# A transformer block on one core: where the second gate's modulation is computed, which engine adds the activation sums, and when weight sums are stored

## The chip, the cores and the metric

The kernel runs on one core of a Trainium2 chip. The core has five engines with their own instruction queues: PE (TensorE, matrix products), DVE (VectorE) and ACT (ScalarE) for elementwise work, POOL (GpSimd), and SP (SyncE), which here issues nearly all transfers between HBM and the on-chip memory (SBUF). Matrix products land in a second memory, PSUM. The metric is the device time of one execution in microseconds (us); less is better. The profile is a hardware trace of one execution.

## The reference

One layer on 512 latent tokens (a grid of 8 rows of 64) and 256 context tokens, 1024 channels, all in 32-bit floats. Cut to what matters here:

```python
mod = silu(c) @ w_ada + b_ada                      # 6 x 1024 values
sh1, sc1, gt1, sh2, sc2, gt2 = split(mod, 6)
h = modulate(rms_norm(x), sh1, sc1)
mix = token_mixer(h, hc, ...)                      # attention, gated linear attention, merge, w_out
x = x + gt1 * mix
h = modulate(rms_norm(x), sh2, sc2)
val, gate = split(h @ w_up, 2)                     # 2 x 2816 columns
gate = depthwise_conv_grid(gate, conv_w, conv_b)   # 3x3 on the 8 x 64 grid
x = x + gt2 * ((gelu(gate) * val) @ w_down)        # 2816 -> 1024
out = rms_norm(x, final_g)
```

`gt2`, the second gate, is needed only where the down projection's result is added.

## The kernel before

**Products.** Every weight and activation of a large product is split into a high part (a cast by ACT, `whi` or `s`) and a low part (the rest, a subtraction, `wlo` or `s`; `split`, line 142, takes POOL unless told otherwise), and three products high-high, high-low, low-high are added up in PSUM (`mm3`). Calls of an engine go through a wrapper, so that nearly all instructions bear line 91 or 90 in the profile; they are told apart by the names of their tiles.

**Stages.** Behind attention and gated linear attention comes the merge (eight steps `j`, from about 405 us): branch projections, gates, and in between the loads of `w_out` (`load_wo`, line 1339). `w_out_norm(t)` (line 1409) then makes the output projection for one of four tiles of 128 tokens, adds it to the residual `x2` and normalises it (`xn`); `transposed(t, xn)` (line 1428) turns it into the columns `h2h`, `h2l`. Then the up projection runs over 22 tiles of 128 hidden columns, tiles 0 to 2 ahead of the loop and 3 to 21 in it, from about 550 to 800 us. The down projection and the last norm follow.

**One tile of the up projection.** `up_weights(i)` (line 1346) loads two pieces of `w_up` (512 KB each, tile `raw`, three buffers) and splits them with POOL (four pairs `whi`, `wlo`). `up_mm` makes 2 x 8 x 3 = 48 products of 512 columns into two PSUM banks, gate and value (`pb`, four in all). `up_out(i)` (line 1476) makes the convolution: one ACT instruction and eight steps on DVE from PSUM into `ac`; then GELU on ACT, and the product with the value half on DVE. Only then are the two banks free for the tile after the next.

**Sums ahead of the down projection.** The down projection of tiles 0 to 17 is done with a scheme of seven products of 2 x 2 blocks. It takes sums and differences of activations and of weights. The activation sums of a pair of tiles are made in `up_out`: one on the even tile in `edge` (one buffer of five pieces of 256), three on the odd tile in `edge` and `second`, all on DVE, and then `edge` is split. The weight sums are made by `weight_sums(n)` (line 1516): two loads of `w_down` into `rawd` (two buffers), two subtractions on DVE, two on POOL; two stores into HBM (`ws`), from where the down projection fetches them. They run at tiles 6, 8, ..., 20 and 21 (`SUM_AT`, line 27), loads and stores in the same tile; `tc.issue_after(load[0].ins)` puts their transfers behind the newest up load on SP's queue.

**The second gate.** `gt2` begins as the bias row in all 128 partitions (line 1470). At tiles 6, 10, 14 and 18 `mod_part` (line 247) makes 256 columns of `silu(c) @ w_ada` as one partial sum in each partition: two loads into `raw`, and eight DVE steps into `mp`. One tile later `mod_bcast` (line 298) adds the 128 partitions on PE with a matrix of ones into a `pb` bank, and DVE adds the result to `gt2`.

**Order.** The program is traced in the order of its text; a planner with a timeline model then orders the instructions of each engine, and each engine runs its list in that order. Work traced earlier has precedence.

Of the kernel before, what the change touches and what calls it, by code (L numbers as in the profile page):

```python
# [23 lines left out]
NF = FF // 128  # L24
NL = 4
NP = (NF - NL) // 2
SUM_AT = [6, 8, 10, 12, 14, 16, 18, 20, 21]
EPS = 1e-6
ATT_SCALE = 96.0 ** -0.5
GQ_SCALE = 128.0 ** -0.5  # L30
# [43 lines left out]
def block_kernel(ctx: ExitStack, tc: tile.TileContext, p, out):  # L74
# [40 lines left out]
    def p2():  # L115
        return tl(psp, [128, 1024], F32, "p2", 2)
# [1211 lines left out]
    hbm = ctx.enter_context(tc.tile_pool(name="hbm", bufs=1, space=bass.MemoryType.DRAM))  # L1328
    x2_ = [tl(hbm, [128, 1024], F32, f"x2_{t}") for t in range(4)]
    sums_ = [tl(hbm, [128, 2048], F32, f"ws_{i}") for i in range(NP)]  # L1330
    emf_ = tc.tile_pool(name="emf", bufs=1)
    emf = emf_.__enter__()
    x2 = [tl(emf, [128, 1024], F32, f"x2{t}") for t in range(4)]
# [4 lines left out]

    def load_wo(k, tile_=raw_tile):
        r = tile_()  # L1340
        SY.dma_start(out=r, in_=w_out[:, k, :])
        h_, l_ = S4([128, 1024]), S4([128, 1024])
        split(h_, l_, r, V if k in (5, 7) else G)
        wo.append((h_, l_))
# [11 lines left out]
    with tc.tile_pool(name="emg", bufs=1) as em_:  # L1356
        def merge_weights(j):
            return (split_w(load_cols(w_in, CGB + j * 128)), split_w(load_cols(w_brg, j * 128, k1=4), 512))

        def mraw():  # L1360
            return tl(em_, [128, 1024], F32, "xn", 3)


        gsum = p2()
        ahead = merge_weights(0)
        for j in range(8):
            wgb, wbg = ahead
            gb = pb()
            proj(wgb, gb)
            if j + 1 < 8:  # L1370
                ahead = merge_weights(j + 1)
            bg = pb()
            for k in range(4):
                bg_ = mm3(bg, k3(wbg[0], 4, 128)[:, k, :], k3(wbg[1], 4, 128)[:, k, :], yT[k][:, 0, :], yT[k][:, 1, :], k == 0,
                    k == 3)
            sg = tl(em_, [128, 512], F32, "sg", 2)
            si = sigmoid(sg, gb)
            tt(V, sg, bg, sg, ALU.mult)
            tt(V, sg, sg, m1[j // 2][:, j % 2, :], ALU.add)
            mg[j] = S4([128, 2, 512])  # L1380
            split(mg[j][:, 0, :], mg[j][:, 1, :], sg, V)
            if j in (1, 2, 3, 5):
                load_wo(len(wo), mraw)
            if j == 0:
                mod_end()
            with tc.issue_after(load[0].ins):
                if j < 4:
                    mod_part(2048 + j * 256, gsum[:, j * 256:j * 256 + 256], mraw)
                elif j == 4:
                    mod_begin(mraw, p2()[:, 0:256])  # L1390
            if j == 6:
                m_, gh, gl = mp_tile(), *[tl(em_, [128, 1024], F32R, "xn", 3) for _ in range(2)]
                with tc.issue_after(si.ins):
                    A.copy(m_, begun[7])
                    A.copy(gh, gsum)
                sub(V, gl, gsum, f(gh))
            elif j == 7:
                with tc.issue_after(bg_.ins):
                    mod_fin(7, m_)
                    gp = p2()  # L1400
                    for half in range(2):
                        hs = slice(half * 512, (half + 1) * 512)
                        total(gp[:, hs], gh[:, hs], gl[:, hs])
                        tt(V, gt1[:, hs], gt1[:, hs], gp[:, hs], ALU.add)
        for k in range(4, 8):
            load_wo(k)
        h2h = [S4([128, 2, 512]) for _ in range(4)]
        h2l = [S4([128, 2, 512]) for _ in range(4)]
        def w_out_norm(t):
            cs = slice(t * 128, (t + 1) * 128)  # L1410
            mp = p2()
            for k in range(8):
                for half in range(2):
                    hs = slice(half * 512, (half + 1) * 512)
                    mm3(mp[:, hs], mg[k][:, 0, cs], mg[k][:, 1, cs], wo[k][0][:, hs], wo[k][1][:, hs], k == 0, k == 7)
            xn = mraw()
            for half in range(2):
                hs = slice(half * 512, (half + 1) * 512)
                tt(V, xn[:, hs], mp[:, hs], gt1[:, hs], ALU.mult)
                tt(V, x2[t][:, hs], x2[t][:, hs], xn[:, hs], ALU.add)  # L1420
            s2 = sm(1, "s2")
            A.activation(xn, x2[t], AF.Square, accum_out=s2)
            A.dma_start(out=x2_[t], in_=x2[t])
            r2 = rstd_exp(s2, 1, 1.0 / D)
            V.tensor_scalar(out=xn, in0=x2[t], scalar1=r2, scalar2=None, op0=ALU.mult)
            return xn

        def transposed(t, xn):
            cs = slice(t * 128, (t + 1) * 128)
            for kk in range(2):  # L1430
                tp = pb()
                for k in range(4):
                    PE.transpose(tp[:, k * 128:(k + 1) * 128], xn[:, (4 * kk + k) * 128:(4 * kk + k + 1) * 128], ident)
                ht = tl(em_, [128, 4, 128], F32, "ht2", 2)
                for k in range(4):
                    kt = 4 * kk + k
                    V.tensor_scalar(out=ht[:, k, :], in0=tp[:, k * 128:(k + 1) * 128], scalar1=modsc2[:, kt:kt + 1],
                                    scalar2=modsh2[:, kt:kt + 1], op0=ALU.mult, op1=ALU.add)
                for k in range(2):
                    split(h2h[2 * kk + k][:, :, cs], h2l[2 * kk + k][:, :, cs], ht[:, 2 * k:2 * k + 2, :], V)  # L1440


        n0 = w_out_norm(0)
        n1 = w_out_norm(1)
        transposed(0, n0)
        n0 = w_out_norm(2)
        transposed(1, n1)
        n1 = w_out_norm(3)
        w0 = [up_weights(i) for i in range(2)]
        z0 = p2()  # L1450
        ps0 = [(z0[:, 0:512], z0[:, 512:1024]), (pb(), pb())]
        up_mm(w0[0], ps0[0], 0, 256)
        transposed(2, n0)
        up_mm(w0[1], ps0[1], 0, 256)
        transposed(3, n1)
        w0.append([])
        for c0 in (FF + 256, 256):
            h_, l_ = S4([128, 1024]), S4([128, 1024])
            split(h_, l_, load_cols(w_up, c0))
            w0[2].append((h_, l_))  # L1460
        z0 = p2()
        ps0.append((z0[:, 0:512], z0[:, 512:1024]))
        up_mm(w0[2], ps0[2], 0, 256)
        for i in range(3):
            up_mm(w0[i], ps0[i], 256, 512)
# [1 line left out]

    emf_.__exit__(None, None, None)
    kept = ctx.enter_context(tc.tile_pool(name="kept", bufs=1))
    gt2 = tl(kept, [128, 1024], F32, "gt2")  # L1470
    SY.dma_start(out=gt2, in_=p["b_ada"][0:1, 5120:6144].broadcast_to([128, 1024]))
    first, second, hid, gelu, edge = [], [], {}, [], [None]

    with tc.tile_pool(name="eff", bufs=1) as ef:

        def up_out(i, ps):
# [23 lines left out]
            elif i % 2 == 0:  # L1500
                edge[0] = tl(ef, [128, 1280], F32, "edge", 1)
                z = grp(edge[0], 5)
                tt(V, z[:, 0::4, :], grp(vp, 2), grp(ac, 2), ALU.mult)
                sub(V, z[:, 2, :], z[:, 0, :], z[:, 4, :])
            else:
                z = grp(edge[0], 5)
                second.append(tl(kept, [128, 768], F32, "second", NP))
                q = grp(second[-1], 3)
                tt(V, q[:, 0::2, :], grp(vp, 2), grp(ac, 2), ALU.mult)
                tt(V, z[:, 1, :], z[:, 4, :], q[:, 2, :], ALU.add)  # L1510
                sub(V, z[:, 3, :], z[:, 1, :], z[:, 0, :])
                sub(V, q[:, 1, :], q[:, 0, :], z[:, 3, :])
                first.append((S4([128, 1024]), S4([128, 1024])))
                split(*first[-1], edge[0][:, 0:1024], V if i > 1 else G)

        def weight_sums(n):

# [1 line left out]
            for i in range(2):  # L1519
                SY.dma_start(out=r[i], in_=w_down[:, 2 * n + i, :])  # L1520
            b11, b12, b21, b22 = [z[:, x:x + 512] for z in r for x in (0, 512)]
            sub(V, b11, b12, b11)
            sub(V, b12, b22, b12)
            sub(G, b22, b22, b11)
            sub(G, b21, b21, b22)
            return r
# [2 lines left out]
            up_out(i, ps0[i])  # L1529
        for i in range(3, NF):  # L1530
            w = up_weights(i)
            if i in (6, 10, 14, 18):
                part = mod_part(5120 + (i - 6) * 64, mp_tile(), raw_tile)
            ps = (pb(), pb())
            up_mm(w, ps, 0, 512)
            up_out(i, ps)

            if i in (7, 11, 15, 19):
                mod_bcast(part, gt2[:, (i - 7) * 64:(i - 3) * 64])
            if i in SUM_AT:  # L1540
                n = SUM_AT.index(i)
                with tc.issue_after(load[0].ins):
                    for k, r in enumerate(weight_sums(n)):
                        SY.dma_start(out=sums_[n][:, k * 1024:k * 1024 + 1024], in_=r)

        raws, fg = [0], tl(ef, [128, 1280], F32, "edge", 1)[:, 0:1024]

# [49 lines left out]
        for n in range(NP):  # L1597
# [12 lines left out]
            if n in (2, 4, 6, 8):  # L1610
                r = load_down(NF - NL + n // 2 - 1)
                wl_.append((S4([128, 1024]), S4([128, 1024])))
                split(*wl_[-1], r)
            if n == NP - 3:
                bw.append(back_weights(0))
        u1, u2, u7, c22 = halves(S4f()), halves(S4f()), halves(S4f()), halves(S4f())
# [141 lines left out]
```

## Time and profile before

| | us |
|---|---|
| time, median of 3 runs | 926.18 (925.3 to 931.43) |
| profiled execution, time | 926.52 |
| profiled execution, span of the trace | 924.7 |
| DVE busy | 703.1 (76% of the span) |
| ACT busy | 409.6 |
| POOL busy | 354.5 |
| PE busy between 557.6 and 802 us | 214.07 of 244.40 |
| DVE busy there | 224.43 of 244.40 |
| POOL busy there | 110.02 of 244.40 |

A row of the trace gives a start, a duration, an engine, an operation, what it writes and reads by tile, and in brackets how long the engine had been idle before it and what it waited for. Groups of instructions give a count, the busy time in us, the mean of one in ns, and the idle time before them. In tables by window the columns are the window, its length, and the busy time and count of PE, weight loads, DVE, ACT and POOL; then the granted PE clock (1.00 is full), the DMA share and the rate.

### The profile page before, as it was taken

The numbers are of one execution on the slowest core, as the hardware profiler recorded it, in microseconds if no ns is written. First come the engines' busy times: TensorE is split into PE (matmuls) and PEld (weight loads), VectorE is DVE, ScalarE is ACT, GpSimd is POOL, SyncE is SP. The second block draws the span as 40 slices with busy tenths as digits, with TensorE's granted clock in tenths as the row PEclk, the third lists the DMA queues.
The fourth block names the chain that finished last, engine by engine and source line by source line (L and its number), as shares of the span: only waits on it lengthen the run. The fifth ranks groups of instructions, "written<-read, shape, count | busy, mean of one in ns | idle before, by whom it ended". The sixth has DMA issues, their size and how long they took to land.

```text
span 924.7 us, 12841 instructions
## 1 busy us (share of the span) xinstructions
PE 875.9 (95%) x4798; PEld 740.7 (80%) x4798; DVE 703.1 (76%) x1089; ACT 409.6 (44%) x664; POOL 354.5 (38%) x220
## 2 busy tenths in 40 slices
PE   7999999999999999999999999996996969999996
PEld 5788899888888888888888998775784858787785
DVE  5487788867877776646746849998989899877857
ACT  4465667745354545345544334232232223355424
POOL 2512373532524343336634234354453444222005
PEclk9999999999999999999999999999897989999998
DMA  9950001152415151449726224645636556557612
GB/s 295 318 148 1 1 12 28 66 143 95 128 35 146 38 148 44 129 147 303 244 86 188 91 78 151 201 131 169 205 138 204 168 153 249 167 190 267 244 33 92
DMA packets 141791, 131.07 MB, mean 142 GB/s; under 512 B 7962, under 2 KB 123010, under 8 KB 141728
## 3 DMA queue, kind: packets, MB, share of 16 engines
q1 hardware_dynamic: 140496, 127.19, 44.7%
q10 hardware_dynamic: 832, 2.40, 0.7%
q8 instruction: 38, 0.62, 0.3%
q0 software_dynamic: 400, 0.65, 0.2%
q14 instruction: 25, 0.20, 0.1%
HBM read 116.39 MB, written 13.63 MB: 141 GB/s over the span
## 4 chain that ended last, share of the span: by engine, by line
PE 63%; DVE 17%; issue 7%; DMA 7%; ACT 3%; POOL 2%; SPq 0%; DVEq 0%; ACTq 0%; POOLq 0%
PE pb L91 27%; PE p L91 17%; PE pb L90 14%; PE p L90 6%; DVE ac L91 5%; DVE mp L91 3%; DMA raw<-in_w_ada_dram 3%; DMA rawd<-in_w_down_dram 2%; DVE s L91 2%; DVE edge L91 2%; DVE second L91 1%; POOL wlo L91 1%; ACT s L91 1%; DMA raw<-in_w_down_dram 1%; DVE wlo L91 1%
## 5 line engine op out<-in xcount | busy, mean ns | idle before, releaser
L91 POOL TENSOR_TENSOR wlo<-raw,whi 128x1024 fp32r<-128x1024 f32 (+1 forms) x88 | 196.4, 2242 | 283.8 <-ACT whi L91 253.4
L91 PE MATMUL pb<-s,whi 128*128 128x512 f32 (+1 forms) x906 | 277.4, 389 | 29.3 <-DVE ac L91 27.9
L91 PEld LDWEIGHTS pb<-s,whi 128*128 128x128 f32 x906 | 169.8, 192 | 65.9 <-issue 31.2
L91 PE MATMUL pb<-s,wlo 128*128 128x512 f32 (+1 forms) x453 | 175.2, 387 | 0.0
L91 ACT CAST whi<-raw 128x1024 fp32r<-128x1024 f32 (+1 forms) x105 | 101.7, 971 | 140.0 <-DMA raw<-in_w_up_dram 42.1
L91 DVE SCALAR_TENSOR_TENSOR ac<-pb,cwT,ac 128x441 f32<-128x441 f32 (+2 forms) x160 | 110.3, 691 | 5.4 <-ACT ac L91 2.3
L90 PE MATMUL pb<-s,whi 128*128 128x512 f32 x320 | 101.1, 394 | 0.0
L91 PEld LDWEIGHTS pb<-s,wlo 128*128 128x128 f32 x453 | 86.6, 191 | 17.1
L91 PE MATMUL p<-s,s 128*128 128x512 f32 (+1 forms) x398 | 84.5, 364 | 2.1 <-DVE s L91 2.0
L91 PEld LDWEIGHTS p<-s,s 128*128 128x128 f32 x398 | 66.9, 189 | 14.7 <-DVE s L91 3.1
L90 PEld LDWEIGHTS pb<-s,whi 128*128 128x128 f32 x320 | 59.3, 188 | 11.5
L90 PE MATMUL pb<-s,wlo 128*128 128x512 f32 x160 | 62.8, 392 | 0.0
L91 ACT ACTIVATE ac<-ac 128x512 f32<-128x512 f32 x22 | 13.9, 632 | 108.7 <-DVE ac L91 108.7
L91 PE MATMUL p<-whi,s 128*128 128x512 f32 x168 | 56.2, 393 | 0.0
L91 POOL TENSOR_TENSOR s<-raw,s 128x1024 fp32r<-128x1024 f32 (+1 forms) x10 | 23.9, 2401 | 80.7 <-ACT s L91 80.7
L91 PE MATMUL pb<-whi,s 128*128 128x512 f32 x164 | 53.7, 390 | 0.0
L91 PE MATMUL pb<-s,s 128*32 128x128 f32 (+2 forms) x340 | 46.3, 319 | 0.9 <-DMA s<-in_w_ada_dram 0.9
L91 DVE TENSOR_TENSOR pl<-pb,ph 128x512 fp32r<-128x512 f32 x48 | 33.0, 687 | 12.7 <-ACT ph L91 12.3
L91 PE MATMUL p<-kT,s 128*128 128x512 f32 (+1 forms) x192 | 41.2, 350 | 0.9 <-ACT P L91 0.9
L91 PEld LDWEIGHTS pb<-s,s 128*128 128x128 f32 (+1 forms) x340 | 36.1, 159 | 6.7 <-DVE rv L91 1.2
L91 DVE SCALAR_TENSOR_TENSOR mp<-raw,csilu,mp 128x256 f32<-128x256 f32 x35 | 35.0, 1001 | 6.4 <-DMA raw<-in_w_ada_dram 6.0
L91 PE MATMUL p<-s,whi 128*128 128x256 f32 (+1 forms) x156 | 38.6, 338 | 0.0
(269 smaller groups left out, 1695.1 us busy)
## 6 DMA issues: line engine op xcount, KB each, us to landing
raw<-in_w_up_dram SPq DMA_DIRECT2D x44, 512.0 KB, 4.8
raw<-in_w_in_dram SPq DMA_DIRECT2D x28, 512.0 KB, 4.1
rawd<-in_w_down_dram SPq DMA_DIRECT2D x21, 512.0 KB, 5.9
s<-in_w_ada_dram SPq DMA_DIRECT2D x20, 512.0 KB, 6.2
raw<-in_w_ada_dram SPq DMA_DIRECT2D x18, 512.0 KB, 6.7
ws<-rawd SPq DMA_DIRECT2D x18, 512.0 KB, 2.6
xn<-in_w_ada_dram SPq DMA_DIRECT2D x10, 512.0 KB, 5.0
raw<-in_w_down_dram SPq DMA_DIRECT2D x9, 512.0 KB, 4.1
```

The lines of the kernel that those rows point to most:

```text
L90: return fn(*args, **kw)
L91: ins = fn(*args, **kw)
```

## The change

The modulation parts of `gt2` leave the up loop. `gt2` is made earlier, in a pool of its own: cleared, with the bias in partition 0 only. `gate_part(j)` loads 2 x 512 KB of `w_ada` into buffers of its own (`wa`, two) and adds eight DVE steps into 256 columns of `gt2`. Part 0 is placed at step 6 of the merge, part 1 behind the last `w_out` loads, parts 2 and 3 between the first token tiles of the output projection. The sum over partitions is made once, in the up loop at tile 12: `gt2` is split and summed by four products (`total`), and ACT copies the result back.

The activation sums go from DVE to POOL; the split of the first pair goes from POOL to DVE. The weight sums are loaded at tiles 4, 6, ..., 20 and stored one tile later; for the first the DVE subtractions go to POOL. The split of the last four down weights goes from POOL to DVE.

```diff
+    gate_ = ctx.enter_context(tc.tile_pool(name="gate", bufs=1))
+    gt2 = tl(gate_, [128, 1024], F32, "gt2")
+    V.memset(gt2, 0.0)
+    SY.dma_start(out=gt2[0:1, :], in_=p["b_ada"][0:1, 5120:6144])
...
     def load_wo(k, tile_=raw_tile):
         r = tile_()
-        SY.dma_start(out=r, in_=w_out[:, k, :])
+        load[0] = SY.dma_start(out=r, in_=w_out[:, k, :])
...
+        def gate_part(j):
+            acc = gt2[:, j * 256:j * 256 + 256]
+            for k0 in (0, 4):
+                r3 = k3(tl(em_, [128, 1024], F32, "wa", 2), 4, 256)
+                SY.dma_start(out=r3, in_=w_ada[:, k0:k0 + 4, 5120 + j * 256:5376 + j * 256])
+                for k in range(4):
+                    V.scalar_tensor_tensor(out=acc, in0=r3[:, k, :], scalar=csilu[:, k0 + k:k0 + k + 1], in1=acc,
+                                           op0=ALU.mult, op1=ALU.add)
...
+            ahead_ = load[0].ins
             if j in (1, 2, 3, 5):
                 load_wo(len(wo), mraw)
             if j == 0:
                 mod_end()
-            with tc.issue_after(load[0].ins):
+            with tc.issue_after(ahead_):
...
+            if j == 6:
+                with tc.issue_after(load[0].ins):
+                    gate_part(0)
         for k in range(4, 8):
             load_wo(k)
+        with tc.issue_after(load[0].ins):
+            gate_part(1)
...
         n0 = w_out_norm(0)
+        gate_part(2)
         n1 = w_out_norm(1)
+        gate_part(3)
         transposed(0, n0)
...
-    gt2 = tl(kept, [128, 1024], F32, "gt2")
-    SY.dma_start(out=gt2, in_=p["b_ada"][0:1, 5120:6144].broadcast_to([128, 1024]))
...
-                sub(V, z[:, 2, :], z[:, 0, :], z[:, 4, :])
+                sub(G, z[:, 2, :], z[:, 0, :], z[:, 4, :])
...
-                tt(V, z[:, 1, :], z[:, 4, :], q[:, 2, :], ALU.add)
-                sub(V, z[:, 3, :], z[:, 1, :], z[:, 0, :])
-                sub(V, q[:, 1, :], q[:, 0, :], z[:, 3, :])
+                tt(G, z[:, 1, :], z[:, 4, :], q[:, 2, :], ALU.add)
+                sub(G, z[:, 3, :], z[:, 1, :], z[:, 0, :])
+                sub(G, q[:, 1, :], q[:, 0, :], z[:, 3, :])
                 first.append((S4([128, 1024]), S4([128, 1024])))
-                split(*first[-1], edge[0][:, 0:1024], V if i > 1 else G)
+                split(*first[-1], edge[0][:, 0:1024], V)
...
-            sub(V, b11, b12, b11)
-            sub(V, b12, b22, b12)
+            sub(V if n else G, b11, b12, b11)
+            sub(V if n else G, b12, b22, b12)
...
-            if i in (6, 10, 14, 18):
-                part = mod_part(5120 + (i - 6) * 64, mp_tile(), raw_tile)
...
-            if i in (7, 11, 15, 19):
-                mod_bcast(part, gt2[:, (i - 7) * 64:(i - 3) * 64])
-            if i in SUM_AT:
-                n = SUM_AT.index(i)
+            if i == 12:
+                gh, gl = split_w(gt2, eng=V)
+                gp = p2()
+                for hs in (slice(0, 512), slice(512, 1024)):
+                    total(gp[:, hs], gh[:, hs], gl[:, hs])
+                A.copy(gt2, gp)
+            n = (i - 4) // 2
+            if 0 <= n < NP:
                 with tc.issue_after(load[0].ins):
-                    for k, r in enumerate(weight_sums(n)):
-                        SY.dma_start(out=sums_[n][:, k * 1024:k * 1024 + 1024], in_=r)
+                    if i % 2 == 0:
+                        made = weight_sums(n)
+                    else:
+                        for k in range(2):
+                            SY.dma_start(out=sums_[n][:, k * 1024:k * 1024 + 1024], in_=made[k])
...
-                split(*wl_[-1], r)
+                split(*wl_[-1], r, V)
```

More of the change, by code (lines that the diff above doesn't have):

```diff
@@ L26 @@
 NP = (NF - NL) // 2
-SUM_AT = [6, 8, 10, 12, 14, 16, 18, 20, 21]
 EPS = 1e-6
```

## The prediction

> **What bounds the kernel now.** I read the first part of the page, then the chain of work that ended last in order of time, then PE's own waits, then the windows and the timeline around one of those waits.
>
> ```profile
> span 924.7 us, 12841 instructions
> ...
> PE 875.9 (95%) x4798; PEld 740.7 (80%) x4798; DVE 703.1 (76%) x1089; ACT 409.6 (44%) x664; POOL 354.5 (38%) x220
> ```
>
> PE (TensorE) is busy for 95% of the span, so the 5% in which it is not are what a change of order can win. In the chain PE alone carries the stretch of the merge; its first long piece also gives the price of one 512-column matmul at full clock, 66.12 / 296 = 0.223 us.
>
> ```profile
> 409.07 66.12 PE pb L91 x296
> ```
>
> One tile of the up projection is 48 such matmuls, 10.7 us; a pair of tiles is 21.4 us. PE's waits between 555 and 802 us, where the up projection runs, have one dominant row:
>
> ```profile
> PE pb L91 <- DVE ac L91: 28.9, 5, 8.9
> ```
>
> Five waits for the depthwise convolution on DVE (VectorE), 28.9 us, the longest 8.9. Windows around them:
>
> ```profile
> 593.00:616.00 23.00, 21.97 (x97) 17.89 (x97) 21.99 (x25) 5.71 (x8) 10.13 (x5) 1.00 0.65 205
> ...
> 649.00:694.00 45.00, 45.00 (x191) 36.91 (x190) 40.83 (x47) 12.47 (x15) 22.58 (x11) 0.95 0.53 176
> ...
> 704.00:749.00 45.00, 45.00 (x188) 36.50 (x189) 41.38 (x48) 13.11 (x16) 22.58 (x11) 0.95 0.53 175
> ...
> 758.50:800.00 41.50, 40.62 (x168) 32.90 (x169) 37.43 (x49) 13.55 (x17) 17.88 (x9) 0.95 0.73 241
> ```
>
> Columns: window, its length, busy time of PE, weight loads, DVE, ACT (ScalarE), POOL (GpSimd), the granted clock, the DMA share, GB/s. The windows begin behind a long wait each (the first behind a short one). PE is full in them, but behind the long waits the granted clock is 0.95 on average where it was 1.00 in the first: a wait costs its idle time and some slow matmuls after it. DVE is at 91 to 96%. Here is how one wait comes about:
>
> ```profile
> 627.97 3.26 SPq L91 DMA_DIRECT2D ws<-rawd  x2
> 638.20 0.38 SPq L91 DMA_DIRECT2D raw<-in_w_ada_dram  x1
> 638.67 9.90 SPq L91 DMA_DIRECT2D raw<-in_w_up_dram  x4
> ...
> 630.84 5.00 POOL L91 TENSOR_TENSOR wlo<-raw,whi 128x1024 fp32r<-128x1024 f32 x2
> 644.93 2.34 POOL L91 TENSOR_TENSOR wlo<-raw,whi 128x1024 fp32r<-128x1024 f32 x1 [9.09 <-ACT whi L91]
> ...
> 631.08 2.50 DVE L91 TENSOR_SCALAR mp<-raw,csilu 128x256 f32<-128x256 f32 x1
> 644.98 2.58 DVE L91 SCALAR_TENSOR_TENSOR mp<-raw,csilu,mp 128x256 f32<-128x256 f32 x1
> ...
> 643.81 1.04 ACT L91 CAST whi<-raw 128x1024 fp32r<-128x1024 f32 x1 [11.39 <-DMA raw<-in_w_up_dram]
> ...
> 648.29 1.19 PE L91 MATMUL pb<-s,whi 128*128 128x512 f32 x2 [8.75 <-DVE ac L91]
> ```
>
> In SP's queue (SyncE's, which issues the loads) the stores of the weight sums stand ahead of the second modulation load, and that ahead of four loads of up weights; so the cast at 643.81 waited 11.39 us for its weights. On DVE the modulation (tile mp) sits among the convolutions. The mp instruction at 644.98 took 2.58 us while a POOL subtraction ran from 644.93 for 2.34; then the convolution ended and PE went on at 648.29. There are four modulation parts in this stage (tiles 6, 10, 14, 18), one per four tiles, and that is the beat of the waits.
>
> **The change, part by part.** The instructions of the stage, grouped by line and form (busy us, mean ns of one), and the page's row for the convolution:
>
> ```profile
> L91 DVE SCALAR_TENSOR_TENSOR ac<-pb,cwT,ac 128x441 f32<-128x441 f32 (+2 forms) x160 | 110.3, 691 | 5.4 <-ACT ac L91 2.3
> ```
>
> ```profile
> L91 DVE SCALAR_TENSOR_TENSOR mp<-raw,csilu,mp 128x256 f32<-128x256 f32 x28 | 31.6, 1130 | 3.2 <-DMA raw<-in_w_ada_dram 2.9
> ...
> L91 DVE TENSOR_TENSOR edge<-edge 128x256 f32<-128x256 f32 x18 | 22.5, 1247 | 0.3
> L91 DVE TENSOR_TENSOR second<-second,edge 128x256 f32<-128x256 f32 x9 | 17.2, 1915 | 0.2
> L91 DVE TENSOR_TENSOR s<-edge,s 128x1024 fp32r<-128x1024 f32 x8 | 13.4, 1669 | 0.0
> L91 DVE TENSOR_SCALAR mp<-raw,csilu 128x256 f32<-128x256 f32 x4 | 7.8, 1957 | 0.0
> L91 DVE TENSOR_TENSOR rawd<-rawd,rawd 128x512 f32<-128x512 f32 x9 | 6.2, 687 | 0.8 <-DMA rawd<-in_w_down_dram 0.8
> ...
> L91 DVE TENSOR_TENSOR edge<-edge,second 128x256 f32<-128x256 f32 x9 | 5.4, 600 | 0.1
> L91 DVE TENSOR_TENSOR edge<-pb,ac 128x512 f32<-128x512 f32 x7 | 4.8, 691 | 2.9 <-ACT ac L91 2.8
> ```
>
> ```profile
> L91 POOL TENSOR_TENSOR wlo<-raw,whi 128x1024 fp32r<-128x1024 f32 x34 | 83.3, 2464 | 75.2 <-ACT whi L91 75.2
> L91 POOL TENSOR_TENSOR rawd<-rawd,rawd 128x512 f32<-128x512 f32 x9 | 12.3, 1371 | 50.1 <-DVE rawd L91 38.6 <-DMA raw<-in_w_up_dram 11.6
> ```
>
> ```profile
> L91 PE MATMUL pb<-mp,ones 128*128 128x256 f32 x8 | 2.4, 387 | 1.0 <-DVE ac L91 1.0
> ```
>
> *Modulation leaves the up stage.* 31.6 + 7.8 = 39.4 us of DVE, eight 512 KB loads on SP, and the broadcasts on PE (2.4 us) go. The waits of 28.9 us are what it leaves on PE. The slow clock behind them: (45 + 45 + 41.5) x 0.05 = 6.6 us. The broadcasts are replaced by four 512-column matmuls at tile 12 (0.9 us): 1.5 us less. Gross gain: 28.9 + 6.6 + 1.5 = 37.0 us.
>
> *Tile 12* adds a cast on ACT, one DVE subtraction (1.2 to 2.1 us by the s<-edge row's mean of 1.67), the matmuls and a copy from PSUM by ACT, and takes one of four weight pairs for a moment. If the weights of tile 13 then come late, that is once, by at most a POOL subtraction of 2.46. Bounds 0 to 3, I take 1: the next tile's weights are normally split ahead.
>
> *Activation sums to POOL.* Per pair DVE loses four 256-wide operations, 2 x 1.25 + 1.92 + 0.60 = 5.0 us. POOL gains four; a 256-wide sum on POOL is not in the trace. The nearest row is the 512-wide one, 1.37 us; the floor by size is half, 0.69. I take 0.75, nearer to the half since the 1024-wide one takes 2.46, so time goes nearly with width. POOL per pair: 4 x 2.46 + 2 x 1.37 + 4 x 0.75 = 15.6 us (18.1 with the upper price), under PE's 21.4. DVE per pair: 16 convolution steps of 0.69 = 11.1, two gate products 1.4, two weight subtractions 1.4, one split 1.7: 15.6 us, also under 21.4. The weight sums of n = 0 and the split of i = 1 swap engines once; they lie beside PE work and cost nothing unless POOL lags.
>
> *Stores a tile later, loads from tile 4 on.* The work is the same, 2 loads and 2 stores per pair; only the stores now find their POOL results done, so the up loads behind them go out at once. Its worth is inside the 28.9. The buffer of a sum is held a tile longer; the next load into it comes a tile after that, so it should not wait.
>
> *What is late next in the up stage.* DVE operations with two inputs in SBUF stretch beside POOL: 2.58 at 644.98, against 0.60 for the mean of the edge<-edge,second row. Three of these remain per pair (two subtractions, the split). At worst each gains about 2 us: 15.6 + 6 = 21.6, just PE's 21.4. So a residue of 0 to 15 us for DVE and POOL waiting on each other over nine pairs; I take 4, near the lower end, as the capacity sums leave 5.8 us per pair free on both engines.
>
> *Modulation arrives in the merge and output projection.* Eight loads in two buffers of its own, and 32 steps on DVE into an SBUF accumulator; part 0 at merge step 6, part 1 behind the w_out loads, parts 2 and 3 between the first tiles of the projection. The stage and its tightest place:
>
> ```profile
> 488.00:499.00 11.00, 11.00 (x51) 9.09 (x50) 5.62 (x7) 5.02 (x8) 10.21 (x4) 1.00 0.63 178
> 499.00:525.00 26.00, 26.00 (x138) 22.29 (x137) 21.97 (x45) 8.32 (x19) 4.95 (x2) 1.00 0.39 128
> 525.00:548.00 23.00, 23.00 (x196) 23.00 (x195) 9.36 (x28) 6.97 (x15) 2.96 (x2) 1.00 0.13 47
> ```
>
> ```profile
> 488.38 7.58 POOL L91 TENSOR_TENSOR wlo<-raw,whi 128x1024 fp32r<-128x1024 f32 x3 [4.58 <-ACT whi L91]
> ...
> 492.74 3.77 DVE L91 TENSOR_TENSOR x<-x,xn 128x512 f32<-128x512 f32 x2
> ...
> 499.01 0.75 DVE L91 TENSOR_SCALAR xn<-x,rr 128x1024 f32<-128x1024 f32 x1
> ```
>
> ```profile
> 501.71 1.03 PE L91 MATMUL pb<-cst,xn 128*128 128x128 f32 x8
> ```
>
> PE is full here, so nothing can be won and something can be lost. DVE has 60 - 37 = 23 us idle in these 60 us, and the 32 steps at 0.60 us (the mean of the nearest 256-wide form that is seldom stretched) are 19 us: they fit, unless they meet POOL. POOL is busy 10.21 of 11 us while the residual of token tile 0 is made (its two additions took 3.77 us). The normalised tile is ready at 499.76 and PE turns it at 501.71: slack 2 us. Modulation steps that fall in ahead of it, each stopped by one of the four POOL subtractions of that window, could delay it by up to 10 us, of which PE would see 8. Below nothing there is no gain, as PE has no idle time here. Bounds 0 to 8, I take 2: the three other token tiles have more room, and part 1's loads stand behind four w_out loads on SP. SP's queue has lead here: the up loads go out from 482.00 on, ahead of the first turn at 501.71, before which PE can use none of them.
>
> ```profile
> 482.00 38.22 SPq L91 DMA_DIRECT2D raw<-in_w_up_dram  x9
> ```
>
> *Split of the last down weights on DVE instead of POOL* (1.7 against 2.5 us, four times): PE is full there, DVE is not; 0.
>
> Sum, against the profiled execution (926.5 us with a span of 924.7; the median of the runs is 926.2): 926.5 - 37.0 + 1 + 4 + 2 = 896.5, rounded to 896.
>
> **Rivals.**
> 1. *The sums bring DVE nothing.* What DVE no longer does, it waits out: its three remaining two-input operations each meet POOL for the full 2 us (21.6 us a pair, above), and the split waits for POOL's last sum on top. Then a pair stays as in 593 to 616, the pair without modulation: 23.0 us against 21.4, and nine pairs lose 14 us instead of 4: 906. For it: DVE was busy 21.99 of 23 us there, and POOL gets busier. Against it: 5.0 us of those leave DVE, and POOL is idle for 5.8 us of a pair. The Trainium skill, SBUF — State Buffer, section "Who interferes with whom", speaks for this rival: a DVE instruction with two SBUF inputs and a GpSimd instruction that reads SBUF shut each other out for the whole instruction, so that sums moved to GpSimd still cost DVE time. The trace agrees for single operations (2.58 us at 644.98, beside POOL's 2.34); by that rule this rival keeps a chance of its own.
> 2. *The output projection pays.* The upper ends there, 8 us, and 3 at tile 12: 926.5 - 37 + 8 + 3 + 4 = 904.
> 3. *The change doesn't do what it says.* The beat of the waits stays because up weights or PSUM come late for another cause: two of the three long waits remain (18 us and 4 of clock): 918, within 1%. Against it: in the windows without modulation PE runs with at most 1.0 us idle in 23.
> 4. *Slower: POOL becomes the bound.* POOL works in order. An activation sum waits for the gate product from DVE, and the weight subtractions queue behind it. POOL's waits for DVE's weight subtractions show the size: 38.6 us, seven times, 5.5 us each.
>
> ```profile
> POOL rawd L91 <- DVE rawd L91: 38.6, 7, 7.5
> ```
>
> With such a wait once in every tile a pair takes 15.6 + 11 = 26.6 us on POOL, 5.2 over PE's 21.4, 47 us over nine pairs: 926.5 - 37 + 3 + 47 = 939. It decides from a wait of 2.9 us a tile on. For it: strict order on POOL. Against it: the sums can stand behind the subtractions, which POOL had 75.2 us of waiting to spare for.
>
> **How the numbers follow.** Likeliest case 0.62, its own range 889 to 901 (all additions zero, to 12 us in all). Rival 1 has 0.14 (to 912 if tile 12 and the projection cost more too), rival 2 has 0.11, rival 3 has 0.07, rival 4 has 0.06. The range is 888 to 912: it takes in the likeliest and rivals 1 and 2 with their spread, some 0.83 of the chance. About 1% is what a measurement of this kernel can tell from no change: the runs shown spread from 925.3 to 931.4. Faster by over 1% (under 917): 0.86; within: 0.08, rival 3 and the mild end of 4; slower: 0.06.
>
> **What would show it.** Right: no PE wait over 3 us between 555 us and the last up tile, granted clock 1.00 there, pairs at about 21.5 us, the weight casts no longer waiting for the up loads, DVE's modulation steps between 455 and 530 with PE still full. Wrong: PE waiting for the low weight parts from POOL (rival 4), DVE's split waiting for POOL (rival 1), a gap of PE ahead of the transposes near 502 us (rival 2), or long waits for the convolution with no modulation near (rival 3).

## The result and the profile after

| | before | after |
|---|---|---|
| time, median (lowest to highest), us | 925.9 (925.3 to 931.43) | 893.81 (892.85 to 896.61) |
| span of the profiled execution, us | 924.7 | 891.1 |
| DVE busy, us | 703.1 | 642.8 |
| POOL busy, us | 354.5 | 374.0 |

The ratio is 0.9646 with a 95% interval of 0.9602 to 0.9689. The forecast was 896 with a range of 888 to 912. Medians and ratios in the following leave out three executions that stand far off the others of their kernels (1237.97, 1760.89 and 3078.14 us).

The page's first part and PE's waits between 440 and 800 us in the changed kernel:

```profile
span 891.1 us, 12819 instructions
...
PE 869.7 (98%) x4794; PEld 738.1 (83%) x4794; DVE 642.8 (72%) x1054; ACT 412.2 (46%) x666; POOL 374.0 (42%) x253
```

```profile
PE pb L90 <- DVE xn L90: 3.7, 1, 3.7
PE p L90 <- DVE wlo L90: 0.8, 1, 0.8
```

The five waits for the convolution (28.9 us) are gone. One new wait of 3.7 us stands in the output projection. The stage from the start of tile 3 (564.5 us), cut into windows of 21.4 us, one pair of tiles each; here the second and the last, and all nine as one:

```profile
586.10:607.50 21.40, 21.40 (x96) 17.74 (x95) 15.48 (x20) 7.77 (x9) 14.33 (x12) 1.00 0.61 197
...
735.90:757.30 21.40, 21.40 (x96) 17.72 (x95) 15.00 (x21) 6.42 (x8) 15.17 (x9) 1.00 0.56 185
...
564.70:757.30 192.60, 192.60 (x851) 159.44 (x850) 140.42 (x191) 69.32 (x82) 137.44 (x88) 1.00 0.58 188
```

The reader is to see 96 products in each of the two windows, PE full and the clock at 1.00. (Nine pairs have 864 products; the trace holds records of 851.) DVE is busy for 140.42 / 9 = 15.6 us of a pair and POOL for 15.3, where the prediction had 15.6 for both. The activation sums on POOL, grouped:

```profile
L90 POOL TENSOR_TENSOR edge<-edge 128x256 f32<-128x256 f32 x18 | 13.3, 739 | 4.1 <-DVE edge L90 3.8
...
L90 POOL TENSOR_TENSOR second<-second,edge 128x256 f32<-128x256 f32 x9 | 7.6, 850 | 0.2
L90 POOL TENSOR_TENSOR edge<-edge,second 128x256 f32<-128x256 f32 x9 | 7.2, 798 | 28.7 <-DVE second L90 16.4 <-DMA rawd<-in_w_down_dram 12.3
```

A sum costs 0.74 to 0.85 us there, against the 0.75 taken. The price of the move shows ahead of this stage, in the timeline of DVE, POOL and PE:

```profile
488.70 4.13 DVE L90 SCALAR_TENSOR_TENSOR gt<-wa,csilu,gt 128x256 f32<-128x256 f32 x8
492.75 1.28 DVE L90 TENSOR_TENSOR xn<-p,s 128x512 f32<-128x512 f32 x2
493.95 2.09 DVE L90 TENSOR_TENSOR x<-x,xn 128x512 f32<-128x512 f32 x1
496.98 1.60 DVE L90 SCALAR_TENSOR_TENSOR gt<-wa,csilu,gt 128x256 f32<-128x256 f32 x1 [0.95 <-DMA wa<-in_w_ada_dram]
498.50 2.88 DVE L90 TENSOR_TENSOR x<-x,xn 128x512 f32<-128x512 f32 x1
...
504.13 2.23 DVE L90 SCALAR_TENSOR_TENSOR gt<-wa,csilu,gt 128x256 f32<-128x256 f32 x1
...
507.40 0.74 DVE L90 TENSOR_SCALAR xn<-x,rr 128x1024 f32<-128x1024 f32 x1
...
493.07 7.75 POOL L90 TENSOR_TENSOR wlo<-raw,whi 128x1024 fp32r<-128x1024 f32 x3 [8.04 <-ACT whi L90]
503.70 2.38 POOL L90 TENSOR_TENSOR wlo<-raw,whi 128x1024 fp32r<-128x1024 f32 x1 [2.87 <-ACT rr L90]
...
508.19 1.97 PE L90 MATMUL pb<-cst,xn 128*128 128x128 f32 x8 [3.71 <-DVE xn L90]
```

Modulation steps (tile gt) stand ahead of and inside the chain that makes the normalised token tile 0: one waits at 496.98 for its load, and those at 496.98 and 504.13 are stretched beside POOL (1.60 and 2.23 us, where the eight from 488.70 on take 4.13 in all). The tile is ready at 508.14, 8.4 us later than before (499.76). PE makes some 11 more products of the projection ahead of the turn than before (100 records where there were 89), then waits 3.7 us for the tile, and behind the wait its granted clock is lower:

```profile
504.50:541.39 36.89, 33.20 (x197) 29.95 (x197) 30.38 (x73) 11.23 (x26) 6.80 (x3) 0.91 0.39 126
```

The first up products behind the four turns began at 534.60 before and begin at 541.39 now, 6.8 us later, of which 3.7 are the wait and the other 3.1 slower products:

```profile
534.60 6.00 PE L91 MATMUL p<-s,s 128*128 128x256 f32 x48
```

```profile
541.39 6.00 PE L90 MATMUL p<-s,s 128*128 128x256 f32 x48
```

So the balance of the change is 33.6 us of span: 6.8 lost ahead of these products, 40.4 won behind them. From there to the end of the span, before and after:

```profile
534.60:924.70 390.10, 349.73 (x1601) 288.94 (x1599) 327.93 (x418) 135.04 (x177) 141.97 (x68) 0.96 0.51 168
```

```profile
541.39:891.10 349.71, 340.26 (x1597) 284.16 (x1595) 253.22 (x350) 137.57 (x179) 161.77 (x101) 0.99 0.53 174
```

PE's idle time fell from 40.4 to 9.5 us, 30.9 less; its busy time fell by 9.5.

### The profile page after: what moved, and what is told of

It reads as the page before. It is cut to its first block, busy times and chain, and to the rows that moved or that the text cites. A ratio compares the mean times of both kernels' runs of the same rounds, so it can differ in the third digit from the quotient of the medians.

```text
span 891.1 us, 12819 instructions
## 1 busy us (share of the span) xinstructions
PE 869.7 (98%) x4794; PEld 738.1 (83%) x4794; DVE 642.8 (72%) x1054; ACT 412.2 (46%) x666; POOL 374.0 (42%) x253
## 4 chain that ended last, share of the span: by engine, by line
PE 80%; DVE 7%; DMA 6%; ACT 4%; issue 2%; POOL 1%; SPq 0%; DVEq 0%; ACTq 0%; POOLq 0%
PE pb L90 42%; PE p L90 17%; PE pb L89 14%; PE p L89 6%; DMA raw<-in_w_ada_dram 2%; DVE s L90 2%; ACT s L90 2%; DMA wa<-in_w_ada_dram 1%; DVE gt L90 1%; DMA s<-ws 1%; DVE wlo L90 1%; DMA xn<-in_w_ada_dram 1%; ACT P L90 1%; DVE mx L90 0%; POOL s L90 0%
## 5 line engine op out<-in xcount | busy, mean ns | idle before, releaser
L90 POOL TENSOR_TENSOR wlo<-raw,whi 128x1024 fp32r<-128x1024 f32 (+1 forms) x88 | 200.7, 2290 | 226.5 <-ACT whi L90 193.2
L90 PE MATMUL pb<-s,whi 128*128 128x512 f32 (+1 forms) x906 | 271.3, 382 | 0.0
L90 PEld LDWEIGHTS pb<-s,whi 128*128 128x128 f32 x906 | 167.3, 188 | 32.3
L90 PE MATMUL pb<-s,wlo 128*128 128x512 f32 (+1 forms) x453 | 172.7, 381 | 0.0
L90 PE MATMUL p<-s,s 128*128 128x512 f32 (+1 forms) x398 | 86.8, 371 | 1.0 <-DVE s L90 0.9
L89 PEld LDWEIGHTS pb<-s,whi 128*128 128x128 f32 x320 | 59.3, 188 | 11.5
L90 POOL TENSOR_TENSOR s<-s,edge 128x512 f32<-128x512 f32 x7 | 12.1, 1759 | 114.7 <-ACT s L90 114.7
L90 ACT CAST ph<-pb 128x512 fp32r<-128x512 f32 x48 | 28.2, 587 | 20.7 <-PE pb L90 20.5
```

The lines of the kernel that those rows point to most:

```text
L89: return fn(*args, **kw)
L90: ins = fn(*args, **kw)
```

## The experiments

The theory at the start: the modulation in the up loop made PE's waits, through DVE's time and through the loads in SP's queue, and its new place costs 6.8 us. The rivals: A, that the activation sums on POOL carried the gain; B, that the later stores did. In the first kernels one part of the change is undone, or done alone.

**Modulation back in the up loop**, all else as changed.

```diff
-        gate_part(2)
...
+            if i in (6, 10, 14, 18):
+                part = mod_part(5120 + (i - 6) * 64, mp_tile(), raw_tile)
...
+            if i in (7, 11, 15, 19):
+                mod_bcast(part, gt2[:, (i - 7) * 64:(i - 3) * 64])
```

> The changed kernel (893.8 us) with the second gate's modulation back in the up loop (tiles 6, 10, 14, 18), all else as changed. Theory (the modulation's DVE steps and its loads in SP's queue made PE's waits): most of the gain goes, the output projection's 6.8 us come back, 905 to 920 us, PE waits for the convolution again once per four tiles. Rival A (the activation sums on POOL carried the gain) and rival B (the later stores carried it): 885 to 895.

Measured: 903.81 us (0.975 of before, 0.973 to 0.977). That is just under the range of the theory and far above the 885 to 895 of the rivals: 10 us of the gain go, not most of it. PE's waits between 556 and 800 us:

```profile
PE pb L90 <- DVE ac L90: 12.2, 3, 5.5
```

The waits are back in their beat, but they are shorter than the 28.9 us with all the sums on DVE. With the modulation in its old place the other parts alone win 22 us against before. The move takes both the steps from DVE and the loads from SP's queue, and no run parts the two. The traces speak for the steps: DVE's own waits for loads of w_ada in the up projection came to 2.9 us before (the mp row in the prediction).

**Activation sums back on DVE**, all else as changed.

```diff
-                sub(G, z[:, 2, :], z[:, 0, :], z[:, 4, :])
+                sub(V, z[:, 2, :], z[:, 0, :], z[:, 4, :])
...
```

> The changed kernel with the four activation sums of a pair back on DVE. Theory: DVE per pair of tiles rises by 5.0 us, from about 16 to about 21 of PE's 21.4, just within, so 893 to 900. Rival A (these sums carried the gain): 905 or more, with PE waiting for the convolution. Rival C (POOL's lock costs as much as it saves): 890 to 893, a little faster than the changed kernel.

Measured: 903.26 us (0.9743, 0.9721 to 0.9765). The expectation of the theory missed: the sums are worth 9 us with the modulation gone. Rival A's 905 isn't reached either, but its sign, PE waiting for the convolution, is there. The nine pairs as one window, and PE's waits:

```profile
564.40:757.00 192.60, 187.22 (x821) 153.19 (x819) 164.86 (x217) 64.40 (x78) 106.61 (x50) 1.00 0.55 174
```

```profile
PE pb L90 <- DVE ac L90: 6.7, 6, 2.7
```

DVE is busy for 164.86 / 9 = 18.3 us of a pair, still under 21.4, and yet PE falls behind in six short waits. The rest of a pair isn't free time: DVE waited 14.8 us in this stage for the loads of w_down ahead of its weight subtractions, and the split took 1.96 us on average. First this kernel, then the changed one:

```profile
L90 DVE TENSOR_TENSOR s<-edge,s 128x1024 fp32r<-128x1024 f32 x9 | 17.6, 1960 | 0.0
...
L90 DVE TENSOR_TENSOR rawd<-rawd 128x512 f32<-128x512 f32 x8 | 5.5, 690 | 14.8 <-DMA rawd<-in_w_down_dram 14.8
```

```profile
L90 DVE TENSOR_TENSOR s<-edge,s 128x1024 fp32r<-128x1024 f32 x9 | 14.2, 1580 | 10.5 <-ACT s L90 10.5
L90 DVE TENSOR_TENSOR rawd<-rawd,rawd 128x512 f32<-128x512 f32 x8 | 7.6, 956 | 1.5 <-DMA rawd<-in_w_down_dram 1.1
...
L90 DVE TENSOR_TENSOR rawd<-rawd 128x512 f32<-128x512 f32 x8 | 6.1, 767 | 20.0 <-DMA rawd<-in_w_down_dram 20.0
```

The changed kernel waits longer for these loads, 20.0 us, and PE doesn't notice: at 15.6 us of a pair DVE has room for it. With the sums back on DVE it has less. Each of PE's six waits ends 12 to 15 us behind such a wait of DVE; the second longest, with the wait of DVE ahead of it:

```profile
698.91 0.69 DVE L90 TENSOR_TENSOR rawd<-rawd 128x512 f32<-128x512 f32 x1 [4.67 <-DMA rawd<-in_w_down_dram]
```

```profile
710.83 0.70 PE L90 MATMUL pb<-s,whi 128*128 128x512 f32 x2 [1.59 <-DVE ac L90]
```

Where the subtraction found its data, as at 678.57, no wait of PE followed. That these waits alone are the cause isn't shown: no run takes them away, and the modulation's move alone (below) has 17.0 us of them and only three waits of PE for the convolution.

**Stores in the tile of their loads**, all else as changed.

```diff
                     if i % 2 == 0:
                         made = weight_sums(n)
-                    else:
                         for k in range(2):
                             SY.dma_start(out=sums_[n][:, k * 1024:k * 1024 + 1024], in_=made[k])
```

> The changed kernel with each pair of stores in the tile of its loads again. Theory: the stores wait for POOL's results at the head of SP's queue and hold back up loads by a few us, which the split-ahead weights cover: 893 to 898. Rival B (the stores carried the gain): 905 or more, ACT's casts waiting for the up loads.

Measured: 890.75 us (0.9612, 0.9589 to 0.9634), under the range of the theory. The median lies 3 us below the changed kernel's, but the intervals overlap; the up projection is full of products as in the changed kernel. Rival B falls here. In the profiled executions PE doesn't wait once behind its first up products here, where in the changed kernel it waits 1.4 us in three places behind the up projection for operands that DVE prepares. Rows of SP's queue show a place where later stores can hurt. First the changed kernel, then this one:

```profile
733.06 14.14 SPq L90 DMA_DIRECT2D raw<-in_w_up_dram  x2
747.29 1.01 SPq L90 DMA_DIRECT2D ws<-rawd  x2
...
752.15 0.33 SPq L90 DMA_DIRECT2D rawd<-ws  x1
```

```profile
739.42 0.33 SPq L90 DMA_DIRECT2D ws<-rawd  x1
742.55 0.33 SPq L90 DMA_DIRECT2D rawd<-ws  x1
```

A store that is put behind the next up loads waits with them for their buffers, and the first down weights of that buffer (rawd from ws) are asked for 9.6 us later. That this makes those waits, or all of the 3 us, was not isolated.

**The modulation's move alone, on the kernel before.**

```diff
+        gate_part(2)
...
-            if i in (6, 10, 14, 18):
-                part = mod_part(5120 + (i - 6) * 64, mp_tile(), raw_tile)
...
+            if i == 12:
+                gh, gl = split_w(gt2, eng=V)
...
```

It ran in two series: 900.7 us (0.9721, 0.9703 to 0.974) and 901.45 (0.9737, 0.972 to 0.9753).

> The kernel before (926 us) with the move of the modulation alone; sums on DVE and stores in the same tile as before. Theory: 39 us of DVE work leave the stage and with them the long waits: 926 - 29 - 7 + 7 for the output projection = about 897, and up to 905 as DVE stays near its limit. Rivals A and B: 920 or more.

> The kernel before with the move of the modulation alone, again, for its profile. Theory: about 901 us, no wait of PE near 9 us left, but short ones as DVE stays near its limit with the sums. Rival (the long waits stay and something else fell): waits of 5 us or more.

PE's waits between 540 and 800 us in the second:

```profile
PE pb L91 <- DVE ac L91: 3.1, 3, 2.5
PE pb L91 <- DVE wlo L91: 1.9, 1, 1.9
```

Three short waits for the convolution are left, as the theory said. The move alone wins 25 us.

**The stores alone, on the kernel before.** Loads from tile 4 on, stores a tile later, and the first two weight subtractions on POOL.

```diff
-            if i in SUM_AT:
-                n = SUM_AT.index(i)
...
+            n = (i - 4) // 2
+            if 0 <= n < NP:
...
```

> The kernel before with the weight sums loaded from tile 4 on and stored a tile later, modulation and activation sums as before. Theory (the stores' place matters only as far as DVE is behind): 915 to 926. Rival B (the stores at the head of SP's queue made the waits): 900 or less. Rival D (later stores only cost): 927 to 930.

Measured: 928.83 us (1.0018, 0.9998 to 1.0038), no difference that the runs can tell. The theory's 915 to 926 is missed; the median lies in rival D's range, but the interval doesn't exclude no change. PE's waits there, and ACT's for the up loads between 556 and 800 us:

```profile
PE pb L91 <- DVE ac L91: 28.3, 5, 8.7
```

```profile
ACT whi L91 <- DMA raw<-in_w_up_dram: 36.0, 4, 11.4
```

They are nearly the same as before (28.9, and 36.7 for ACT). The stores at the head of SP's queue, one of the causes in the prediction's reading of the wait at 648 us, made neither PE's waits nor the late up loads. The activation sums alone, on the kernel before, were not run; that they carry the 22 us of the first experiment follows from this one only as the rest.

**No modulation parts at all**: the changed kernel without `gate_part`, so the second gate is the bias alone.

```diff
-        gate_part(2)
         n1 = w_out_norm(1)
-        gate_part(3)
...
```

> The changed kernel (893.8 us) without its four modulation parts: the 8 loads of w_ada and 32 DVE steps for the second gate are left out, so the gate is the bias alone. Theory (these steps delay the normalised token tile 0 and cost the output projection 6.8 us): 886 to 888, no PE wait ahead of the first turn. Rival (the 6.8 us come from elsewhere, such as the order of the first turn): 892 to 895.

Measured: 887.61 us (0.959, 0.9563 to 0.9618). The turn of token tile 0:

```profile
501.43 1.03 PE L90 MATMUL pb<-cst,xn 128*128 128x128 f32 x8
```

It is back at its old time (501.71) with no wait, and the first up products begin at 534.33. The steps and loads of the modulation cost all of the 6.8 us.

**Modulation placed where DVE is idle.** Part 1's loads go one w_out load earlier, parts 2 and 3 behind the turns of token tiles 2 and 3; DVE's steps are held behind the last step of the turn (those of parts 0 and 1 behind the newest gate of the merge).

```diff
+                with tc.issue_after(load[0].ins):
+                    SY.dma_start(out=r3, in_=w_ada[:, k0:k0 + 4, 5120 + j * 256:5376 + j * 256])
                 for k in range(4):
+                    with tc.issue_after(step[0].ins):
...
             load_wo(k)
+            if k == 6:
+                gate_part(1)
...
         transposed(2, n0)
+        gate_part(2)
...
         transposed(3, n1)
+        gate_part(3)
```

> The changed kernel with part 1's loads one w_out load earlier and parts 2 and 3 behind the turns of token tiles 2 and 3; nothing left out. Theory: the steps lie where DVE is idle, PE's wait ahead of the first turn goes: 886 to 889. Rival: the late steps delay the first convolutions, or the wait only moves: 892 or more.

Measured: 890.87 us (0.9633, 0.9602 to 0.9665), between the ranges of the theory and of the rival. The wait ahead of the turn is gone, but it has moved, as the rival had it, and two waits of 1.6 and 1.4 us came behind the first up products. The wait that moved:

```profile
486.15 19.03 PE L90 MATMUL p<-s,s 128*128 128x512 f32 x82 [2.85 <-DVE s L90]
```

Part 1's steps now stand on DVE ahead of the low part of a w_out weight, which began at 480.18 in the changed kernel and begins at 484.87 here; PE's products go on as it ends:

```profile
478.76 2.48 DVE L90 SCALAR_TENSOR_TENSOR gt<-wa,csilu,gt 128x256 f32<-128x256 f32 x1
481.16 2.88 DVE L90 TENSOR_TENSOR s<-sg,s 128x512 fp32r<-128x512 f32 x1
483.96 0.99 DVE L90 SCALAR_TENSOR_TENSOR gt<-wa,csilu,gt 128x256 f32<-128x256 f32 x2
484.87 1.22 DVE L90 TENSOR_TENSOR s<-raw,s 128x1024 fp32r<-128x1024 f32 x1
```

**The same, and the stores in the tile of their loads.**

```diff
                     if i % 2 == 0:
                         made = weight_sums(n)
-                    else:
                         for k in range(2):
...
```

> As v2_gate_fit, and the stores in the tile of their loads. Theory: both gains add, 3 us below v2_gate_fit: 883 to 887. Rival (the 3 us of the store's place were chance): as v2_gate_fit.

Measured: 887.53 us (0.9595, 0.957 to 0.9621), just above the range and 3.3 below the kernel with the stores a tile later. In a direct comparison on one chip:

> The changed kernel again, for a direct comparison on one chip: 893 to 896 by all theories.

> w_fit_same again beside the changed kernel. Theory (the modulation steps placed where DVE is idle and the stores in the tile of their loads are both real gains): 5 to 8 us below c_after. Rival (chips and chance): within 2 us.

The changed kernel: 894.09 us (0.9665, 0.9631 to 0.9699). The other: 888.38 us (0.9587, 0.9571 to 0.9604). The intervals don't meet; 5.7 us are won over the changed kernel.

**Activation sums made twice on POOL.**

```diff
+                for _ in range(2):
+                    sub(G, z[:, 2, :], z[:, 0, :], z[:, 4, :])
...
```

> The changed kernel with each of the four activation sums of a pair made twice on POOL: POOL per pair goes from 15.3 to about 18.4 us of PE's 21.4. Theory (POOL has room, its order does no harm): 893 to 898. Rival 4 of the prediction (waits in POOL's order decide): 905 or more.

Measured: 896.24 us (0.9688, 0.9664 to 0.9711). The nine pairs as one window:

```profile
564.00:756.60 192.60, 192.60 (x856) 159.65 (x855) 139.76 (x185) 69.03 (x83) 157.44 (x124) 1.00 0.57 183
```

POOL works 157.44 / 9 = 17.5 us of a pair and PE is still full: POOL's order does no harm in these nine pairs at this load. Right behind them PE waits once for a convolution, and then twice for low weight parts (1.27 and 1.34 us, where the changed kernel has 0.8 in one wait):

```profile
763.93 0.70 PE L90 MATMUL pb<-s,whi 128*128 128x512 f32 x2 [1.92 <-DVE ac L90]
```

These waits are of the size of the 2.4 us between the medians; whether the doubled sums make them wasn't followed.

## Why the prediction was right, point by point

**The bound and the mechanism.** Right. PE's waits in the up projection came from DVE's work between the convolutions. With the modulation alone gone from there 3.1 of the 28.9 us are left, and with the whole change PE is full and at clock 1.00, as the prediction said the profile would show. DVE's and POOL's time for a pair came out as in the sums. Of the causes that it read at 648 us, the stores fell; the share of the modulation's loads, apart from its steps, stays open.

**Gross gain, 37.0 us.** Behind the first up products 40.4 us were won, 3.4 more. PE's idle time fell by 30.9 where the term had 28.9: two further waits of 0.7 us stood beside that row, and some 0.8 us of waits went behind the up projection. PE's busy time fell by 9.5 where the term had 6.6 + 1.5 = 8.1 for the slow clock and the broadcasts.

**Whose gain it is.** Mis-read. The prediction gave all of it to the modulation's leaving; its sum has no term for the activation sums. The modulation alone wins 25 us, the other parts without it 22, all together 32. They are two ways to the same end: DVE needs room, and either gives most of it. The third part, the stores a tile later, was said to have its worth inside the 28.9 us; alone it wins nothing, and with the modulation gone the kernels with stores in their old place were 2.6 to 3.3 us faster by the medians, in three pairs of kernels (with the modulation as changed, with it placed where DVE is idle, and with the sums on DVE; the two of the last pair differ in the small swaps of engine too).

**The residue of 4 us in the up projection, and 1 us at tile 12.** None showed: no wait of PE in the nine pairs, tile 12 among them. Rival 1 is answered by the sums' undoing: DVE did gain by their move. The Trainium skill, SBUF — State Buffer, section "Who interferes with whom", stood behind that rival. The stretching it tells of is in the trace (the split on DVE takes 1.58 us on average and 1.23 at its shortest, the gate steps up to 2.23), but it did not eat the gain: POOL's sums are short (0.74 to 0.85 us), and DVE has 5.8 us a pair to wait in. Which of the two counts wasn't tested.

**The output projection, 2 us within 0 to 8.** Mis-sized: 6.8, near the upper end, and by the mechanism of rival 2. The prediction had the slack of 2 us and the POOL window right; it chose the low value because part 1's loads stood behind the w_out loads and the other token tiles had more room. In the run part 1's eight steps stand right ahead of the chain (from 488.70), and part 2's, counted at eight steps a part, inside it, the first of them (at 496.98) behind a wait for its load. The prediction's sign for rival 2, a gap of PE ahead of the turn, is what the trace shows, and of the 6.8 us only 3.7 are the gap; the prediction priced no slower clock behind it.

**Rival 4.** It didn't come, and doubling the sums on POOL didn't bring it (896.24 us, where it needed 905 or more).

**The sum.** The forecast was 30.0 us off the profiled execution, 896.5; the profiled execution of the changed kernel takes 892.85. Behind the first up products 40.4 us were won where the sum had 37.0 - 1 - 4 = 32.0; ahead of them 6.8 were lost where it had 2. The two errors, 8.4 and 4.8, stand against each other, and 3.6 are left. That the total was closer than its terms is luck.

## What to carry to other kernels

A wait that comes in the beat of one job need not be that job's alone. Here DVE was near its limit, and taking either of two jobs off it removed most of the wait; so the parts of a change are not to be added up. Work that is moved into a stage where the matrix engine is full has only its slack there to hide in, and that slack is read from the chain that feeds the next product, not from the idle time of the stage.

An engine at 18.3 of 21.4 us was not yet covered here, where it also waits in order for loads; a sum of durations under the limit isn't enough.

## What the runs showed of the hardware that was not expected

With the sums on POOL, POOL is busy for 71% of the nine pairs (137.44 of 192.60 us), where it had 50% of the windows behind the long waits before (22.58 of 45). DVE's remaining operations with two inputs in SBUF slowed only a little: the two weight subtractions of a pair rose from 687 and 686 to 956 and 767 ns on average, while the split fell from 1669 to 1580, some 0.3 us more a pair in all. The means moved both ways; where on the timeline the two engines meet would explain that, but it wasn't followed.
